# A plain output projection, kept up-projection operands, and down-projection operands made earlier

## The chip, the core and the metric

The kernel runs on one core of a Trainium2 chip. A core has a matrix engine (TensorE, PE in the rows; PEld is its loading of weights), three engines for elementwise work (VectorE or DVE, ScalarE or ACT, GpSimd or POOL), a sequencer SP that issues the DMAs here, and 16 DMA engines that move data between device memory and the on-chip memory SBUF. Matrix products land in PSUM, a small accumulator memory. Each engine runs its own list of instructions in order; semaphores tie them together. The metric is the time of one execution on the device in microseconds (us); lower is better.

## The reference

One encoder layer on two sequences, 512 and 2048 tokens of width 1024, all in fp32. The mixer concatenates four branches to a width of 1024; the change begins behind it:

```python
mix = jnp.concatenate([o_a, o_b, o_c, o_d], axis=-1)
return mix @ w_out                                        # (T, 1024) @ (1024, 1024)

def _conv_ffn(x, w_up, conv_w, conv_b, w_down):
    h = x @ w_up                                          # 1024 -> 2 * 2816
    hp = jnp.pad(h, ((0, 0), (1, 1), (0, 0)))
    h = hp[:, :-2] * conv_w[0] + hp[:, 1:-1] * conv_w[1] + hp[:, 2:] * conv_w[2] + conv_b
    gate, val = jnp.split(h, 2, axis=-1)
    return (jax.nn.gelu(gate) * val) @ w_down             # 2816 -> 1024

x = _layer_norm(ALPHA * x + mix, ln1_g, ln1_b)
x = _layer_norm(ALPHA * x + _conv_ffn(x, ...), ln2_g, ln2_b)
```

## The kernel before

**Split products.** A factor in fp32 is split into a high part, rounded to the matmul's input type (`hi`, on ACT), and a low part, the rest (`split`, line 131, on POOL or DVE). A product is three matmuls: high by high, high by low, low by high.

**Seven products for eight.** Output projection, up- and down-projection cut both factors into 2 x 2 blocks and form seven block products instead of eight. This needs sums and differences of blocks on both sides (`s1` to `s4`, `t1` to `t4`) and combination steps on the results. Each operand, a "unit" of 128 x 1024 (512 high and 512 low columns, 512 KB), is split on its own.

**Stages and order.** Order on each engine is not as written: a planner simulates the program and gives each engine the instruction of the highest priority (program order) that is ready, so work written later fills idle engines earlier. The order it finds is fixed in the program. All DMAs concerned are issued by SP.

1. Attention (`mla`), over 64 units of the sample and 16 of the prompt. At sample head two it calls `load_wout`; at steps 49, 67, 69, 81 and 82 of the loop in `build` the generator `outproj_head` makes more units of w_out and the first pair of mix tiles.
2. `outproj`: ten pairs of 128-token tiles. `mix_ops` loads two tiles of the mixed activations, forms four sums and differences, and splits seven operands into a ring of buffers (`op_ring`). `project` runs seven products of 12 matmuls (line 1141), with combination steps on DVE, ACT and POOL between them (`scaled`, line 1147), and `norm` does the layer norm. Operands of w_out stand in the ring "w" (12 slots) and in arena slots.
3. `ffn_up`: three blocks of tokens (`FF_BLOCKS`: 896, 896 and 768 tokens; seven products of 450, 450 and 386 columns). At each block's start `operands` makes B and T from the layer-normed x2 (through the two "xs" buffers). Then for each of 22 feature tiles f, `weights(f)` loads two 512 KB pieces of w_up, forms `s1` to `s4` (POOL, DVE; line 1209), and splits seven units into "w"; `features` runs 84 matmuls (lines 1313 to 1315), PSUM evacuation on DVE and ACT, the convolution (`conv`, lines 1319 to 1321), the gelu and the product (1354), and stores g. All of `weights` is done again in each block.
4. `ffn_down`: six chunks of w_down, 4 units in the first, 14 in the others, run through twice, each time for five pairs of token tiles (start offsets of 0 or 1 chunk). In the first pass `weights` (with `plain_units`, and `plain_weights` in `down_head`) makes the units from w_down and stores them to the scratch tensor `wdops`; in the second pass `again` loads them. `gate` loads and splits the activations g of the next job; `product` has the matmuls (line 1530).

Of the kernel before, what the change touches and what calls it, by code (L numbers as in the profile page):

```python
# [9 lines left out]
F32 = mybir.dt.float32  # L10
# [23 lines left out]
TOK0 = (2048, 0)  # L34
XW = 900
# [66 lines left out]
class Builder:  # L102
# [65 lines left out]
    def build(self):  # L168
        tc, nc, I = self.tc, self.nc, self.I
        with tc.tile_pool(name="cst", bufs=1, reuse_waits="tile") as cst, tc.tile_pool(name="scr", bufs=1, space=bass.MemoryType.DRAM) as scr:  # L170
# [34 lines left out]
            self.wd = self.t(scr, [NF // 2, 7, P, D], "wdops")  # L205

            with tc.tile_pool(name="arena", bufs=1, reuse_waits="tile") as self.A:
# [11 lines left out]
                with tc.tile_pool(name="mls", bufs=2, reuse_waits="tile") as ms:  # L219
# [8 lines left out]
                    for i, _ in enumerate(mla):  # L228
                        if i in (49, 67, 69, 81, 82):
                            next(head)  # L230
# [811 lines left out]
    def wout_units(self, k, js, units, lo_eng="pool"):  # L1042
        H = D // 2
        add = self.add
        wo = self.I["w_out"][0].rearrange("(k p) (a n) -> p k a n", p=P, a=KD)
        load = lambda h: self.wraw(wo[:, h * KD // 2 + k]).rearrange("p k n -> p (k n)")
        r1 = load(0) if js != (4,) else None
        r2 = load(1)
        b21, b22 = r2[:, :H], r2[:, H:]
        x = {4: b21, 6: b22}  # L1050
        if r1 is not None:
            b11, b12 = r1[:, :H], r1[:, H:]
            t1, t2, t3 = [self.t(self.wr2, [P, H], "s", bufs=4) for _ in range(3)]
            add("pool", t1, b12, b11, ALU.subtract)
            add("dve", t2, b22, t1, ALU.subtract)
            if 0 in js:
                add("pool", t3, b22, b12, ALU.subtract)
                x.update({0: b11, 1: t2, 2: t1, 3: t3})
            else:
                add("pool", t3, b21, t2, ALU.subtract)  # L1060
                x[5] = t3
        for j in js:
            u = units()
            self.split(x[j], u[:, :H], u[:, H:], "act", "dve" if lo_eng == "mix" and j % 2 == 0 else "pool")
            self.wout[k, j] = u

    def halves(self, slots, shape):
        for i in slots:
            t = self.a(i, [P, 2, D], F32R)
            for h in range(2):  # L1070
                yield t[:, h].rearrange(shape[0], **shape[1]) if shape else t[:, h]

    def load_wout(self):
        self.wout = {}
        self.wslot = self.halves((10, 12, 11, 9, 0, 5, 3, 4), None)
        for k in range(3):
            self.wout_units(k, (0, 1, 2, 3), lambda: self.wtile().rearrange("p k n -> p (k n)"))

    def mix_ops(self, p):
        KH = KD // 2  # L1080
        add = self.add
        raw = []
        for t in (2 * p, 2 * p + 1):
            s, i = (1, t) if t < 16 else (0, t - 16)
            raw.append(self.wraw(self.mix[s].rearrange("(k p) t -> p k t", p=P)[:, :, i * P:(i + 1) * P]))
        a11, a12, a21, a22 = raw[0][:, :KH], raw[0][:, KH:], raw[1][:, :KH], raw[1][:, KH:]
        s1, s2, s3, s4 = [self.t(self.wr2, [P, KH, P], "s", bufs=4) for _ in range(4)]
        add("pool", s1, a21, a22, ALU.add)
        add("dve", s2, s1, a11, ALU.subtract)
        add("pool", s3, a11, a21, ALU.subtract)  # L1090
        add("dve", s4, a12, s2, ALU.subtract)
        for i, x in enumerate((a11, s2, s1, s3, a12, a22, s4)):
            o = next(self.ops)
            self.split(x, o[:, 0], o[:, 1], "act", "pool" if i in (0, 4) else "dve")
            yield o

    def op_ring(self):
        KH = KD // 2
        while True:
            for tag in ("xs", "xs", "wraw2", "wraw2"):  # L1100
                yield self.t(self.wr2, [P, 2, KH, P], tag, F32R, bufs=2)
            yield from self.halves((7, 8, 2), ("p (h k e) -> p h k e", dict(h=2, k=KH)))

    def outproj_head(self):
        self.ops = self.op_ring()
        self.wout_units(3, (0, 1, 2, 3), lambda: next(self.wslot), "pool")
        yield
        for k in range(KD // 2):
            self.wout_units(k, (4,), lambda: next(self.wslot), "pool")
        yield  # L1110
        self.first = self.mix_ops(0)
        self.G0 = list(self.first)
        yield
        for k in range(KD // 2):
            self.wout_units(k, (5, 6), lambda: next(self.wslot), "mix")
            if k % 2:
                yield

    def outproj(self, head):
        nc, I, pp, add = self.nc, self.I, self.pp, self.add  # L1120
        H, KH = D // 2, KD // 2
        with self.tc.tile_pool(name="p3", bufs=2, reuse_waits="tile") as sp:
            G = {0: self.G0}
            place = lambda t: (1, t) if t < 16 else (0, t - 16)

            def fetch(p):
                P1[p] = self.t(sp, [P, H], "p1")
                x = self.a((1, 6)[p % 3 - 1], [P, 2, D]) if p % 3 else self.t(sp, [P, 2, D], "x", bufs=1)
                for h in range(2):
                    s, i = place(2 * p + h)  # L1130
                    self.load(x[:, h], self.y1[s][i * P:(i + 1) * P])
                return x
            P1 = {}
            X = {0: fetch(0)}
            next(head, None)
            W = self.wout

            def product(ps, G, i, first, last):
                for k in range(KH):
                    u = W[k, i]  # L1140
                    mm = lambda a, b, st, sp_: nc.tensor.matmul(ps, a, b, start=st, stop=sp_, skip_group_check=True)
                    mm(G[i][:, 0, k], u[:, :H], first and k == 0, False)
                    mm(G[i][:, 0, k], u[:, H:], False, False)
                    mm(G[i][:, 1, k], u[:, :H], False, last and k == KH - 1)

            def scaled(a, ps):
                nc.vector.scalar_tensor_tensor(a, a, ALPHA, ps, op0=ALU.mult, op1=ALU.add)

            def norm(t, x, late):
                s, i = place(t)  # L1150
# [4 lines left out]
                add("pool" if late else "dve", x, x, g_bc, ALU.mult)  # L1155
# [3 lines left out]
            def project(p):  # L1159
                x, g = X.pop(p), G.pop(p)  # L1160
                (x11, x12), (x21, x22) = [(x[:, h, :H], x[:, h, H:]) for h in range(2)]
                a, b, c = [self.t(pp, [P, 512], tag, bufs=n) for tag, n in (("s", 3), ("t", 3), ("o", 2))]
                e = "pool" if p < NP - 1 else "dve"
                product(a, g, 0, True, False)
                p1 = P1.pop(p)
                nc.scalar.copy(p1, a)
                product(b, g, 1, True, False)
                scaled(x12, b)
                product(c, g, 2, True, False)
                product(b, g, 3, False, False)  # L1170
                scaled(x22, b)
                add(e, x12, x12, p1, ALU.add)
                scaled(x21, p1)
                product(a, g, 4, False, True)
                scaled(x11, a)
# [495 lines left out]
```

## Time and profile before

| | us |
|---|---|
| three runs, median | 3377.93 |
| lowest and highest | 3365.83, 3380.04 |
| the profiled execution, whole | 3381.85 |
| its span, first to last instruction | 3379.5 |

| engine | busy us | share of the span |
|---|---|---|
| PE | 3164.6 | 94% |
| PEld | 2733.5 | 81% |
| DVE | 2486.9 | 74% |
| POOL | 2158.8 | 64% |
| ACT | 1526.9 | 45% |

DMA moved 405.84 MB, 120 GB/s on average. [...] A listed matmul duration overlaps the next ones, so the rate is read from the distance of starts. The shares are means over stages, so the stages are read one by one: 1315 to 1580 us is the output projection, 1583 to 1984, 1984 to 2387 and 2388 to 2774 us are the three feature blocks, and from about 2775 us on the down-projection runs.

### The profile page before, as it was taken

Reading aid. Unit: us, or ns where it says so; the run is one execution under the profiler, and the core shown is the slowest. Engines: PE = TensorE matmul, PEld = TensorE weight load, DVE = VectorE, ACT = ScalarE, POOL = GpSimd, SP = SyncE. Lnnn points to the kernel's source line nnn. Section 1 sums busy time; section 2 is a strip of 40 time slices with the busy share of each in tenths; the row PEclk is TensorE's granted clock in tenths of the full one; section 3 lists DMA queues with packets and bytes.
Section 4 is the critical chain, followed back from the end, with each engine's and each line's share of the span. In section 5 each row is a group of like instructions: output and inputs, shape, how many; then the busy total and the mean of one; then the engine's idle time right before and its main releaser. Section 6 shows DMA issues by size and latency. Waiting matters only on the chain. (4 is left out here: it accounts for less than half of the span.)

```text
span 3379.5 us, 45596 instructions
## 1 busy us (share of the span) xinstructions
PE 3164.6 (94%) x15999; PEld 2733.5 (81%) x15999; DVE 2486.9 (74%) x4000; ACT 1526.9 (45%) x2765; POOL 2158.8 (64%) x1651
## 2 busy tenths in 40 slices
PE   7899999799999997987999999999899988999997
PEld 6788878677889996765899979999799986777885
DVE  6332216676888887898788788887788778989768
ACT  3212215455677766333444454444444443444224
POOL 6322222345766657666888868888688868885546
PEclk9999999777999998998999999999899999999998
DMA  6222143523211004344322232222232248557653
GB/s 216 95 79 88 55 143 124 180 78 100 84 29 30 26 18 138 132 151 139 89 90 90 90 101 86 88 93 87 90 97 91 87 174 308 214 194 286 231 197 111
DMA packets 358465, 405.84 MB, mean 120 GB/s; under 512 B 42840, under 2 KB 286392, under 8 KB 356700
## 3 DMA queue, kind: packets, MB, share of 16 engines
q1 hardware_dynamic: 358236, 402.93, 36.0%
q8 instruction: 126, 2.06, 0.2%
q14 instruction: 103, 0.84, 0.1%
HBM read 269.02 MB, written 133.84 MB: 119 GB/s over the span
## 5 line engine op out<-in xcount | busy, mean ns | idle before, releaser
L131 POOL TENSOR_TENSOR w<-s,w 128x512 fp32r<-128x512 f32 x281 | 460.8, 1649 | 144.0 <-ACT w L121 140.3
L131 POOL TENSOR_TENSOR w<-wraw,w 128x512 fp32r<-128x512 f32 x189 | 277.9, 1479 | 42.5 <-ACT w L121 39.4
L1313 PE MATMUL t<-T,w 128*128 128x450 f32 (+1 forms) x792 | 286.9, 365 | 18.3 <-DVE u L1209 18.2
L1313 PE MATMUL s<-B,w 128*128 128x450 f32 (+1 forms) x792 | 286.2, 363 | 6.7 <-DVE h L1209 5.7
L1314 PE MATMUL t<-T,w 128*128 128x450 f32 (+1 forms) x792 | 286.9, 362 | 0.0
L1315 PE MATMUL t<-T,w 128*128 128x450 f32 (+1 forms) x792 | 286.8, 362 | 0.0
L1314 PE MATMUL s<-B,w 128*128 128x450 f32 (+1 forms) x792 | 286.1, 361 | 0.2 <-DVE B L131 0.2
L1315 PE MATMUL s<-B,w 128*128 128x450 f32 (+1 forms) x792 | 285.5, 360 | 0.0
L121 ACT CAST w<-wraw 128x512 fp32r<-128x512 f32 x225 | 138.2, 617 | 240.2 <-PE t L1315 142.8
L1320 DVE SCALAR_TENSOR_TENSOR h<-h,convc,h 128x896 f32<-128x896 f32 (+1 forms) x132 | 207.1, 1583 | 53.4 <-ACT h L1319 53.4
L1321 DVE SCALAR_TENSOR_TENSOR h<-h,convc,h 128x896 f32<-128x896 f32 (+1 forms) x132 | 239.9, 1839 | 0.0
L121 ACT CAST w<-s 128x512 fp32r<-128x512 f32 x299 | 183.5, 619 | 112.4 <-PE s L1315 54.9
L924 DVE TENSOR_SCALAR_CACHE_REDUCE a<-s,low 128x512 f32<-128x512 f32 x272 | 195.1, 745 | 31.7 <-PE t L952 23.9
L139 PE MATMUL mm<-xTl,a 128*128 128x512 f32 x520 | 205.7, 396 | 1.5 <-DVE xTl L131 1.5
L1530 PE MATMUL t<-w,go 128*128 128x512 f32 x696 | 195.8, 400 | 11.3 <-DVE xs L1371 4.8
L140 PE MATMUL mm<-xTh,a 128*128 128x512 f32 x520 | 201.7, 391 | 0.0
L138 PE MATMUL mm<-xTh,a 128*128 128x512 f32 x520 | 198.0, 394 | 1.4 <-ACT xTh L121 0.7
L131 DVE TENSOR_TENSOR a<-t,a 128x512 fp32r<-128x512 f32 x240 | 160.6, 682 | 32.5 <-ACT a L121 32.0
L1313 PEld LDWEIGHTS t<-T,w 128*128 128x128 f32 x792 | 151.5, 191 | 33.6 <-DVE u L1209 22.9
L940 POOL TENSOR_SCALAR a<-a,mrc 128x2048 f32<-128x2048 f32 (+1 forms) x80 | 140.0, 1752 | 49.5 <-DVE mrc L939 49.4
L121 ACT CAST a<-t 128x512 fp32r<-128x512 f32 x240 | 135.1, 586 | 79.7 <-PE t L952 74.5
L952 PE MATMUL t<-ident,a 128*128 128x128 f32 x1088 | 159.9, 278 | 10.1 <-DVE a L131 5.4
(412 smaller groups left out, 9574.7 us busy)
## 6 DMA issues: line engine op xcount, KB each, us to landing
wraw<-in_w_up_dram SPq DMA_DIRECT2D x132, 512.0 KB
w<-wdops SPq DMA_DIRECT2D x54, 512.0 KB
wdops<-w SPq DMA_DIRECT2D x50, 512.0 KB
graw<-g SPq DMA_DIRECT2D x100, 256.0 KB
g<-h SPq DMA_DIRECT2D x44, 448.0 KB
x<-x SPq DMA_DIRECT2D x24, 512.0 KB
wdops<-wd SPq DMA_DIRECT2D x24, 512.0 KB
wd<-wdops SPq DMA_DIRECT2D x24, 512.0 KB
```

Of the source, the lines that this page charges most:

```text
L121: nc.scalar.copy(out, src)
L131: e.tensor_tensor(lo, src, hi.bitcast(F32), op=ALU.subtract)
L138: mm(ps, wh, xh, start=first, stop=False)
L139: mm(ps, wh, xl, start=False, stop=False)
L140: mm(ps, wl, xh, start=False, stop=last)
L924: nc.vector.tensor_scalar(e[:, c * 512:c * 512 + 512], ps, 1.0, self.low, op0=ALU.mult, op1=ALU.max, accum_out=m4[:, c:c + 1])
L1313: mm(ps[:, :hw], a, xh[:, k, :hw], start=first and k == 0, stop=False, skip_group_check=True)
L1314: mm(ps[:, :hw], a, xl[:, k, :hw], start=False, stop=False, skip_group_check=True)
L1315: mm(ps[:, :hw], b, xh[:, k, :hw], start=False, stop=last and k == KH - 1, skip_group_check=True)
L1320: nc.vector.scalar_tensor_tensor(c[:, :n], hb[:, 1:n + 1], cw[:, 1, ft:ft + 1], c[:, :n], op0=ALU.mult, op1=ALU.add)
L1321: nc.vector.scalar_tensor_tensor(c[:, :n], hb[:, 2:n + 2], cw[:, 2, ft:ft + 1], c[:, :n], op0=ALU.mult, op1=ALU.add)
L1530: mm = lambda a, b, st, sp_: nc.tensor.matmul(ps, a, b, start=st, stop=sp_, skip_group_check=True)
```

## The change

- *Output projection.* Plain: `load_wout` loads eight pieces of w_out and splits sixteen units (twelve in "w", four in arena slots 10 and 12). `mix_ops(t)` loads one tile and splits it in two halves, high on ACT, low on DVE and POOL, into one of three arena slots. `project(t)` does 2 x 8 x 3 matmuls in two PSUM banks and one scaled sum for each. The head runs at steps 81 and 82 only.
- *Up-projection.* In block one `weights` also stores five of its seven units (1, 2, 3, 5, 6) to a new scratch tensor `wuops`. In blocks two and three `weights_again` loads these five into "w", and splits only units 0 and 4, from one loaded piece of w_up.
- *Down-projection operands.* The generator `down_ops` makes the 74 units of w_down in blocks two and three, two for each feature tile, through the two "xs" buffers, high on ACT, low on POOL, and stores them to `wdops`. `ffn_down` and `down_head` load units from there in both passes.

```diff
 def load_wout(self):
+    rest = self.halves((10, 12))
+    for k in range(KD):
+        raw = flat(self.wraw(wo[:, k]))
+        for h in range(2):
+            u = flat(self.wtile()) if k < 6 else next(rest)
+            self.split(raw[:, h * H:(h + 1) * H], u[:, :H], u[:, H:], "act", "pool")
+            self.W[k, h] = u
 def mix_ops(self, t):
+    raw = self.wraw(self.mix[s].rearrange("(k p) t -> p k t", p=P)[:, :, i * P:(i + 1) * P])
+    o = self.a((8, 9, 11)[t % 3], [P, 2, KD, P], F32R)
+    for h in range(2):
+        ks = slice(h * KD // 2, (h + 1) * KD // 2)
+        self.split(raw[:, ks], o[:, 0, ks], o[:, 1, ks], "act", ("dve", "pool")[h])
 def project(t):
+    for h in range(2):
+        for k in range(KD):
+            u = W[k, h]
+            self.mm3(ps[h], g[:, 0, k], g[:, 1, k], u[:, :H], u[:, H:], k == 0, k == KD - 1)
+        a = x[:, h * H:(h + 1) * H]
+        nc.vector.scalar_tensor_tensor(a, a, ALPHA, ps[h], op0=ALU.mult, op1=ALU.add)
+    norm(t, x)
 def weights(f):
+    if i in KEPT:
+        self.store(self.wu[f, KEPT.index(i)], u.bitcast(F32).rearrange("p k n -> p (k n)"))
+def weights_again(f):
+    g = self.wraw(wup[:, :, f * P:f * P + P])
+    for i in range(7):
+        u = self.wtile()
+        if i in KEPT:
+            self.load(u.bitcast(F32).rearrange("p k n -> p (k n)"), self.wu[f, KEPT.index(i)])
+        else:
+            h = slice(0, KH) if i == 0 else slice(KH, KD)
+            self.split(g[:, h], u[:, :KH], u[:, KH:], "act", "pool")
 for f in range(NF):
-    W = weights(f)
+    W = weights_again(f) if bi else weights(f)
+    if bi:
+        next(down_ops, None)
+        next(down_ops, None)
+def down_ops(self):
+    for k in range(FH):
+        for h in range(2):
+            raw.append(self.t(self.wr2, [P, KD, P], "wraw2", bufs=2))
+            self.load(raw[h], self.wdown(h * FH + k))
...
+            add("pool", t1, b12, b11, ALU.subtract)
+            add("dve", t2, b22, t1, ALU.subtract)
+            add("pool", t3, b22, b12, ALU.subtract)
+            add("dve", t4, b21, t2, ALU.subtract)
+        for i, x in enumerate((b11, t2, t1, t3, b21, t4, b22) if k else (b11, b12, b21, b22)):
+            o = self.t(self.wr2, [P, D], "xs", F32R, bufs=2)
+            self.split(x, o[:, :H], o[:, H:], "act", "pool")
+            self.store(self.wd[k, i], o.bitcast(F32))
+            yield
 def prepare(i):
+    for k in chunks[i % NC]:
+        for j in range(7 if k else 4):
+            got[i, k, j] = self.down_unit(unit(), k, j)
+            yield
```

## Rows read from the trace of the kernel before

**Rows 1.** Busy time by stage: stretch, length, PE, PEld, DVE, ACT, POOL, PEclk, DMA.

```profile
1345.00:1582.00 237.00, 203.10 (x815) 158.29 (x814) 211.11 (x270) 74.80 (x123) 148.98 (x83) 0.93 0.44 147
...
1620.00:1984.00 364.00, 363.75 (x1775) 332.56 (x1774) 301.69 (x264) 170.41 (x258) 297.15 (x187) 1.00 0.28 88
1984.00:2024.00 40.00, 32.99 (x146) 26.25 (x145) 27.57 (x54) 21.87 (x40) 26.93 (x22) 0.83 0.41 125
2024.00:2387.00 363.00, 362.07 (x1764) 330.89 (x1763) 300.20 (x266) 167.66 (x255) 294.82 (x185) 1.00 0.28 88
...
2428.00:2754.00 326.00, 306.98 (x1677) 303.14 (x1676) 261.67 (x249) 150.78 (x248) 276.29 (x175) 0.97 0.29 87
2754.00:2830.00 76.00, 59.25 (x254) 47.72 (x252) 59.70 (x77) 27.34 (x58) 49.55 (x43) 0.89 0.86 330
2830.00:3110.00 280.00, 266.73 (x1115) 209.92 (x1114) 259.56 (x397) 125.16 (x295) 221.12 (x214) 0.99 0.67 242
3110.00:3330.00 220.00, 220.00 (x946) 177.33 (x945) 162.35 (x279) 72.58 (x185) 122.78 (x150) 1.00 0.54 195
```

**Rows 2.** Timeline of PE, output projection: start, us, instruction, count, [idle before <-releaser].

```profile
1315.78 2.86 PE L1141 MATMUL s<-w,xs 128*128 128x512 f32 x9
...
1371.32 2.97 PE L1141 MATMUL t<-a,wraw 128*128 128x512 f32 x12
...
1379.67 2.27 PE L1141 MATMUL s<-w,a 128*128 128x512 f32 x9
...
1574.49 5.49 PE L1141 MATMUL o<-a,a 128*128 128x512 f32 x12 [3.81 <-DVE x L1371]
```

**Rows 3.** Waits of PE, 1345 to 1582: us in total, times, longest.

```profile
PE t L1141 <- DVE x L1147: 11.5, 4, 9.6
```

**Rows 4.** Groups of DVE, 1330 to 1590: busy us, mean ns | idle before.

```profile
L131 DVE TENSOR_TENSOR a<-s,a 128x512 fp32r<-128x512 f32 x23 | 29.5, 1282 | 0.0
L1371 DVE TENSOR_TENSOR a<-a,ln1g 128x1024 f32<-128x1024 f32 x12 | 20.2, 1682 | 5.3 <-ACT a L1154 5.2
L152 DVE BATCH_NORM_STATS2 ln1st<-a 128x6 f32<-128x512 f32 x24 | 15.8, 682 | 0.2
...
L1147 DVE SCALAR_TENSOR_TENSOR a<-a,t 128x512 f32<-128x512 f32 x12 | 8.1, 675 | 3.9 <-PE t L1141 3.9
```

**Rows 5.** Timeline of SP's DMA issues, start of the attention and its end.

```profile
862.86 2.61 SPq L113 DMA_DIRECT2D wraw<-in_w_out_dram  x2
...
1294.58 2.29 SPq L113 DMA_DIRECT2D wraw<-mix  x2
```

**Rows 6.** 1303 to 1345: all engines, then line 1141 alone.

```profile
1303.00:1345.00 42.00, 30.69 (x153) 25.61 (x152) 31.39 (x56) 23.19 (x49) 30.84 (x29) 0.83 0.42 133
...
1303.00:1345.00 42.00, 12.93 (x41) 9.54 (x42) 0.83 0.42 133
```

**Rows 7.** Groups of POOL and DVE in 18 feature tiles of block three, 2441.9 to 2739.0.

```profile
L131 POOL TENSOR_TENSOR w<-s,w 128x512 fp32r<-128x512 f32 x72 | 119.3, 1667 | 32.6 <-ACT w L121 32.6
...
L1209 POOL TENSOR_TENSOR s<-wraw,wraw 128x512 f32<-128x512 f32 x18 | 27.1, 1506 | 0.8
...
L1209 DVE TENSOR_TENSOR s<-wraw,s 128x512 f32<-128x512 f32 x18 | 23.1, 1285 | 14.8 <-POOL w L131 14.8
```

**Rows 8.** Timeline of PE in block three, a run and a pause.

```profile
2550.21 0.34 PE L1313 MATMUL t<-T,w 128*128 128x386 f32 x1
...
2554.63 0.34 PE L1313 MATMUL t<-T,w 128*128 128x386 f32 x1
...
2559.38 0.57 PE L1313 MATMUL t<-T,w 128*128 128x386 f32 x1 [2.30 <-DVE u L1209]
```

**Rows 9.** Busy time: 10 us after that pause; 30 us of the down-projection's start.

```profile
2560.00:2570.00 10.00, 10.00 (x50) 10.00 (x50) 5.44 (x7) 4.00 (x6) 7.78 (x6) 0.85 0.45 138
...
2790.00:2820.00 30.00, 23.94 (x86) 17.46 (x85) 24.82 (x30) 7.99 (x21) 24.97 (x24) 0.80 1.03 412
```

**Rows 10.** Waits of ACT, 1600 to 2780: us in total, times, longest.

```profile
ACT w L121 <- PE t L1315: 171.4, 99, 5.8
```

More of the change, by code (lines that the diff above doesn't have):

```diff
@@ L34 @@
 TOK0 = (2048, 0)
+KEPT = (1, 2, 3, 5, 6)
 XW = 900
@@ L228, in build @@
                     for i, _ in enumerate(mla):
-                        if i in (49, 67, 69, 81, 82):
-                            next(head)
+                        if i in (81, 82):
+                            next(head, None)
                 self.outproj(head)
@@ L1040, in wraw, with load_wout, halves @@
         return raw
-    def wout_units(self, k, js, units, lo_eng="pool"):
+    def load_wout(self):
         H = D // 2
-        add = self.add
+        self.W = {}
         wo = self.I["w_out"][0].rearrange("(k p) (a n) -> p k a n", p=P, a=KD)
[L1046 to L1067, printed above, removed]
+        flat = lambda a: a.rearrange("p k n -> p (k n)")
+        rest = self.halves((10, 12))
[5 more added lines that the diff above has]
+                self.W[k, h] = u
+    def halves(self, slots):
         for i in slots:
@@ L1070, in halves @@
             for h in range(2):
[L1071 to L1102, printed above, removed]
-    def outproj_head(self):
[L1105 to L1117, printed above, removed]
+                yield t[:, h]
@@ new lines, in place, with mix_ops @@
+    def place(self, t):
+        return (1, t) if t < 16 else (0, t - 16)
+    def mix_ops(self, t):
+        s, i = self.place(t)
+        raw = self.wraw(self.mix[s].rearrange("(k p) t -> p k t", p=P)[:, :, i * P:(i + 1) * P])
[3 more added lines that the diff above has]
+            self.split(raw[:, ks], o[:, 0, ks], o[:, 1, ks], "act", ("dve", "pool")[h])
+        return o
+    def outproj_head(self):
+        self.G = {}
+        for t in range(2):
+            self.G[t] = self.mix_ops(t)
+            yield
@@ L1119, in outproj @@
     def outproj(self, head):
         nc, I, pp, add = self.nc, self.I, self.pp, self.add
-        H, KH = D // 2, KD // 2
+        H = D // 2
         with self.tc.tile_pool(name="p3", bufs=2, reuse_waits="tile") as sp:
[L1123 to L1150, printed above, removed]
@@ L1154, in norm @@
                 nc.scalar.activation(x, x, AF.Identity, bias=nr, scale=r)
-                add("pool" if late else "dve", x, x, g_bc, ALU.mult)
+                add("dve", x, x, g_bc, ALU.mult)
                 add("pool", x, x, b_bc, ALU.add)
                 self.store(self.x2[s][i * P:(i + 1) * P], x)
[L1159 to L1175, printed above, removed]
-                add(e, x22, x22, p1, ALU.add)
-                add("dve", x22, x22, c, ALU.add)
-                product(b, g, 5, False, True)
-                add("dve", x21, x21, b, ALU.add)
-                product(c, g, 6, False, True)
-                add("dve", x12, x12, c, ALU.add)
-                for h in (1, 0):
-                    norm(2 * p + h, x[:, h], p == NP - 1)
@@ L1191, in outproj @@
+            fetch(0)
+            for t in range(NT):
+                if t + 1 < NT:
+                    fetch(t + 1)
+                    if t + 1 not in G:
+                        G[t + 1] = self.mix_ops(t + 1)
+                if t == 0:
                     g_bc = self.t(sp, [P, D], "ln1g", bufs=1)
@@ L1361, in ffn_up @@
             meta = {}
+            down_ops = self.down_ops()
             for bi in range(len(FF_BLOCKS)):
@@ L1404, in down_head @@
         wr2 = self.wr2
-        self.head_w = self.plain_weights(self.wtile)
+        self.head_w = [self.down_unit(self.wtile(), 0, i) for i in range(4)]
         raw = self.t(wr2, [P, 2, 1, 2 * P], "wraw2", bufs=2)
```

90 lines of the change are left out of this document (27 added, 63 removed).

## The prediction

> **What bounds the kernel now.** I read the busy time by stage first, since the share over the whole span hides which stage is limited by what. The reader should see two kinds of stage [rows 1]. In feature blocks one and two (1620 to 1984, 2024 to 2387) and in the second pass of the down-projection (3110 to 3330) PE is busy all the time at full clock: only fewer or shorter matmuls would help there. In the output projection (1345 to 1582), block three (2428 to 2754) and the first pass of the down-projection (2830 to 3110) PE has holes, at a mean clock under 1, while DVE or POOL is at 80 to 94%. Only these three can pay for the change.
>
> To price the holes I take the matmul pitch from the timeline. A listed duration overlaps its neighbours, so I use starts: 36 matmuls of 512 columns take 1379.67 - 1371.32 = 8.35 us, 0.232 us each [rows 2]. In block three (386 columns) 25 matmuls take 2554.63 - 2550.21 = 4.42 us, 0.177 us each [rows 8]. A stage's loss is its length less count times pitch.
> - Output projection: 840 x 0.232 = 195 us of matmuls, between a first group at 1315.8 and an end at 1574.49 + 5.49 = 1580.0 [rows 2].
> - Block three: 326 - 1677 x 0.177 = 29 us lost [rows 1].
> - Down-projection, first pass: 280 - 1115 x 0.232 = 21 us lost; second pass: 220 - 946 x 0.232 = 0.5 us [rows 1].
>
> Who is late: in the output projection PE's longest waits are for DVE, 9.6 us [rows 3] and 3.8 us before the last group [rows 2]; DVE has 211 us of work in 237 [rows 1]. In block three the chain is one step longer. POOL does nine operations of 128x512 a feature tile (seven low parts, two sums) at 1.5 to 1.7 us: 13.6 to 15.0 us, against 84 x 0.177 = 14.9 us of matmuls; with what it waits for, 18 tiles take 297 us, 16.5 us a tile. DVE's two differences wait for POOL (14.8 us in the 18 tiles) [rows 7], the PSUM evacuation stands behind them on DVE, and PE waits 2.3 us for it, after which a matmul is listed with 0.57 us instead of 0.34 [rows 8].
>
> **The change, part by part.**
>
> *Plain output projection.* Seven products become eight: 20 tiles x 2 halves x 8 x 3 = 960 matmuls instead of 840, so +120 x 0.232 = +27.8 us on the engine that is the bound nearly everywhere. Against that stands what leaves DVE. A plain tile asks of it two scaled sums from PSUM (0.675), two statistics (0.682), one gain (1.68), one low half (1.28) and some small ones [rows 4]: 5.7 us and a little, against 48 x 0.232 = 11.1 us of matmuls. Six of seven combination steps, the four operand differences a pair and most low parts are gone; POOL, at 149 of 237 us [rows 1], loses work too. So I expect this stage to be bound by PE, without holes.
>
> Its start: the 16 weight operands are asked for at head two of the attention, but the planner runs such work far ahead; the loads of w_out begin at 862.9 [rows 5]. The old ones took eighteen POOL operations (twelve low parts, six differences) and three of DVE; the new ones take sixteen low parts on POOL and none of DVE. So it is nothing; the two saved, some 3 us, are one end, and the other, if planned worse, as much again. The operand units made in the attention's tail go. The first mix columns are loaded at 1294.6 [rows 5]; a tile needs only a load and two splits. By my estimate that is some 8 us, so that products begin at 1303; the ends are 1.3 us for 512 KB at the rate of [rows 9] and a split of 1.3 us [rows 4], and the 21 us that the old units took from there to the first group at 1315.8 [rows 2]. From 1303 to 1345 PE is busy 30.7 us, of which 41 projection matmuls take 41 x 0.232 = 9.5 us [rows 6]: 21 us of attention remain. End: 1303 + 21 + 960 x 0.232 = 1547, against 1580: -33. I take **-30**, for a pause or two. Bounds: -33 - 5 with the early start, -20 with the late one, and +28 if the old holes stay.
>
> *Into each block.* Each f = 0 takes some 20 us more than a tile, because DVE, ACT and the x2 loads make the operands B and T (1984 to 2024: PE 33 of 40 us, clock 0.83) [rows 1]. This work stays. It gains from fewer splits beside it, and loses because the x2 loads now share two "xs" buffers and the queue with stores. I take **0**, -3 to +6 for each of three.
>
> *Block one* gets five stores of 512 KB a tile. They need SP and the DMA engines, both with room (88 GB/s, share 0.28 [rows 1]); a slot of the 12-slot ring "w" is free only when its store has landed too, but the product that frees it comes later anyway. **0**; behind a store on SP stand the next raw loads, a tile ahead, so a delay under some 15 us costs nothing.
>
> *Blocks two and three.* Five of seven operands come by load, two are split from one raw half; two units of w_down are made a tile. POOL a tile: 2 + 2 low parts and 4/7 of a sum, 4.6 operations x 1.6 = 7.3 us instead of 13.6 to 15.0. DVE loses two differences and gets 4/7 of one. Block two is at PE's limit already: **0**. Block three's holes come from POOL, so they go: **-28** of 29. What is late next there is PE itself; DVE has 262 us in 326 [rows 1] and loses more than a tenth of it. Bounds: -29, 0.
>
> The change adds waits here. SP's loads into "w" wait for PE to release a slot. Behind them stand the g stores, the stores of w_down units and raw loads; ACT (line 1319, which reuses the "h" buffer of a g store; and the casts into "xs", two buffers, each free when its store has landed) waits for those. A slot is reused twelve products later, 12 x 12 x 0.177 = 25 us in block three: that is the cover, and its failing is the slow rival below.
>
> DMA volume a tile in block three: 0.5 MB raw w_up, 2.6 operands, 1.0 stores, 0.3 w_down, 0.4 g = 4.9 MB, over 14.9 us 330 GB/s; in block two, over 17.3 us, 287. The trace shows 412 GB/s for 30 us with PE at work beside it [rows 9], so it fits.
>
> *Down-projection.* Its first pass makes no operands any more: 14 loads a chunk replace four raw loads, splits and 14 stores. That is the second pass's work, which loses 0.5 us. I take **-18** of 21; the rest are epilogues. Bounds: -21, 0. At the start (2754 to 2830, PE 59 of 76 us at 330 GB/s [rows 1]) fourteen operand loads now go ahead of the gate loads, where two raw pairs stood; 6 more loads of 512 KB at 412 GB/s [rows 9] are 7.6 us, against splits saved: **0**, -10 to +12.
>
> **Sum.** -30 - 28 - 18 = -76 us. The profiled execution took 3381.85 us (span 3379.5), so 3306; it lies 3.9 us above the median of the three, 3377.93, so the forecast for a median is **3302 us**.
>
> **The rivals.**
> - *The matmuls are added, the holes stay.* Plain tiles still wait (small DVE operations, the mix loads). For: the stage is not in this form in the trace. Against: DVE would be half idle. +28 instead of -30: 3360.
> - *Block three and the first pass keep their holes*, because DVE, not POOL, set them. For: PE's waits name DVE [rows 8]. Against: DVE's own waits there name POOL [rows 7]. +46: 3348.
> - *DMA becomes the bound.* The planner bunches the w_down units, since POOL is free: at seven a tile in block two, 8.3 MB a tile, at 412 GB/s [rows 9] 20.2 us against 17.3, 2.9 us for each of 74/7 = 10.6 tiles: +31, 3333. [...]
> - *Slower: ACT stands still for a store.* Each of the 74 units casts into one of two "xs" buffers; ACT runs in order, and the copies that PE's next product on the bank needs stand behind the cast. If the store is late (SP is behind a load that waits for PE), PE pauses. Price of one pause: 2.3 us [rows 8] and the slower matmuls after it (50 in 10 us where 10/0.177 = 56 fit [rows 9]), 1.1 us: 3.4 us. From 76/3.4 = 22 of 74 pauses on the gain is gone; with half of them, +126: 3428. For: ACT waits 171 us for PE at the same casts already [rows 10]. Against: those waits, up to 5.8 us, leave blocks one and two without a loss [rows 1]. [...]
> - *The change doesn't do what it says*: the loads come too late to replace the splits. It is the slow rival's cousin, priced within it.
>
> **How the numbers follow.** Forecast 3302 (own range 3280 to 3325, from the bounds of transitions and start): 0.60. DMA-bound, 3333: 0.09. Holes kept in block three and first pass, 3348: 0.09. Holes kept in the projection, 3360: 0.07. Transitions and start gain too, 3302 - 9 - 10 = 3283 or somewhat less: 0.06. Slow, 3428: 0.09. The range that leaves out 2 in 10 is 3268 to 3350. Over 0.5% (17 us, about what a measurement of this kernel tells from no change) faster is below 3361: 0.85 (half of the case at 3360 among it). Same, the rest of that case and the tail of the one at 3348: 0.06. Slower: 0.09.
>
> **What would show it.** Output projection: some 960 matmuls, 223 us of them, at clock 1, DVE under 65%. Block three: 14.9 us a tile, POOL under 55%, no wait of PE for DVE over 1 us. First pass: PE over 98%. Wrong would be: PE waits on line 1313 in blocks two and three with ACT's casts into "xs" waiting for DMA; a DMA share of 1 in block two with PE holes; PE waits for mix loads or DVE in the projection; a first f of a block over 42 us.

## The result

The changed kernel takes 3291.48 us (median of 4 runs, 3286.28 to 3299.96), the kernel before 3378.98 (median of 4, 3365.83 to 3380.87): a ratio of 0.9752, 95% interval 0.9718 to 0.9785, 87.5 us less. The forecast was 3302, with a range of 3268 to 3350. The profiled execution of the changed kernel took 3299.96 us (span 3298.2, mean granted clock of TensorE 0.962 of full speed; before 0.953), the longest of its four; by the prediction's sum it should have been 3306.

In the profiles, the attention's first score matmul starts at 847.7 us before and at 852.7 after. In the profiles of the runs below, whose edits all lie behind it, it starts between 837.0 and 846.8. What happens ahead of it says nothing on the change, so I take times from that matmul on (starts of matmuls in the timelines of PE; for the projection the end of its last one):

| from the first score matmul to | before | after | difference | this step | predicted |
|---|---|---|---|---|---|
| the projection's end | 732.3 | 688.9 | -43.4 | -43.4 | -30 |
| second feature tile of block one | 772.0 | 735.9 | -36.1 | +7.3 | 0 |
| block two | 1136.7 | 1099.8 | -36.9 | -0.8 | 0 |
| its second tile | 1175.0 | 1133.5 | -41.5 | -4.6 | 0 |
| block three | 1540.0 | 1498.3 | -41.7 | -0.3 | 0 |
| its second tile | 1579.3 | 1541.4 | -37.9 | +3.8 | 0 |
| its last up-projection matmul | 1926.6 | 1857.0 | -69.6 | -31.7 | -28 |
| the end of the span | 2531.8 | 2445.4 | -86.4 | -16.8 | -18 |

These are two profiles, and single steps vary between profiles of the same code. In three runs below that keep the old projection it ends at 726.2 to 727.1 us, and in the runs with the plain one (but for one that puts work into the attention) at 686.0 to 688.9, so its step is -37 to -46. The first feature tile of block one, 37.2 and 45.2 us here, takes 34.8 to 35.0 and 44.1 to 46.3 us there.

The changed kernel by stage, the stages of [rows 1] and [rows 6] again (stretch, length, busy us and count of PE, PEld, DVE, ACT and POOL, granted clock of TensorE as a share of full speed, DMA share, GB/s):

```profile
1303.00:1345.00 42.00, 42.00 (x228) 35.98 (x227) 22.54 (x54) 17.93 (x37) 8.53 (x11) 0.98 0.28 88
1345.00:1541.00 196.00, 196.00 (x843) 157.83 (x842) 98.85 (x166) 51.41 (x77) 73.95 (x39) 1.00 0.47 153
1541.00:1589.00 48.00, 31.95 (x161) 25.81 (x160) 30.60 (x64) 22.69 (x45) 32.98 (x27) 0.82 0.71 216
1589.00:1952.00 363.00, 363.00 (x1774) 332.62 (x1773) 289.05 (x262) 166.51 (x252) 284.54 (x181) 1.00 0.69 242
1952.00:1986.00 34.00, 27.82 (x131) 22.44 (x130) 20.31 (x42) 20.06 (x37) 23.23 (x22) 0.90 0.62 203
1986.00:2351.00 365.00, 365.00 (x1782) 334.21 (x1782) 231.16 (x240) 138.02 (x194) 152.87 (x98) 1.00 0.82 290
2351.00:2394.00 43.00, 31.25 (x134) 25.36 (x133) 19.97 (x43) 18.24 (x36) 20.28 (x20) 0.72 0.50 155
2394.00:2710.00 316.00, 316.00 (x1785) 315.26 (x1784) 192.69 (x231) 116.86 (x178) 107.03 (x73) 1.00 0.86 300
...
2760.00:3030.00 270.00, 264.62 (x1117) 210.70 (x1116) 211.16 (x362) 102.22 (x248) 151.75 (x174) 0.99 0.65 233
3030.00:3250.00 220.00, 219.12 (x940) 176.10 (x939) 161.42 (x279) 72.00 (x180) 117.78 (x144) 1.00 0.54 192
```

The reader is to see PE busy without a hole, at clock 1.00, in the projection (196 of 196 us, DVE at 50% instead of 89) and in block three (316 of 316, POOL at 34% instead of 85). What is left are three short stretches, the first f of each block, where PE is busy for 32 of 48, 28 of 34 and 31 of 43 us at clocks from 0.72 to 0.90. PE's waits there, at the start of block one and then of block three (us in total, times, longest):

```profile
PE s L1258 <- DVE B L132: 6.4, 1, 6.4
PE t L1198 <- DMA xs<-x: 5.9, 1, 5.9
PE o L1198 <- DVE o L1196: 2.1, 1, 2.1
...
PE t L1198 <- DMA xs<-x: 7.9, 3, 3.8
PE o L1198 <- DMA xs<-x: 3.0, 4, 2.1
PE t L1257 <- ACT T L122: 0.9, 1, 0.9
```

### The profile page after: what moved, and what is told of

The parts are those of the page before. It is cut to its first block, busy times and chain, and to the rows that moved or that the text cites. A ratio compares the mean times of both kernels' runs of the same rounds, so it can differ in the third digit from the quotient of the medians.

```text
span 3298.2 us, 45978 instructions
## 1 busy us (share of the span) xinstructions
PE 3152.9 (96%) x16119; PEld 2739.0 (83%) x16119; DVE 2130.4 (65%) x3770; ACT 1390.7 (42%) x2493; POOL 1617.3 (49%) x1329
## 4 chain that ended last, share of the span: by engine, by line
PE 84%; DVE 6%; DMA 5%; ACT 2%; issue 2%; SPq 1%; POOL 1%; DVEq 0%; ACTq 0%; POOLq 0%
PE s L1257 6%; PE s L1258 6%; PE s L1259 6%; PE t L1452 6%; PE t L1257 5%; PE t L1258 5%; PE t L1259 5%; PE s L139 4%; PE s L1452 4%; PE s L140 4%; PE s L141 4%; PE o L1452 4%; PE t L954 3%; PE mm L141 3%; PE mm L140 3%; PE mm L139 3%
## 5 line engine op out<-in xcount | busy, mean ns | idle before, releaser
L132 POOL TENSOR_TENSOR w<-wraw,w 128x512 fp32r<-128x512 f32 x162 | 235.5, 1459 | 315.1 <-ACT w L122 269.4
L1258 PE MATMUL t<-T,w 128*128 128x450 f32 (+1 forms) x792 | 283.8, 358 | 0.0
L1259 PE MATMUL t<-T,w 128*128 128x450 f32 (+1 forms) x792 | 283.7, 358 | 0.0
L1257 PE MATMUL t<-T,w 128*128 128x450 f32 (+1 forms) x792 | 282.1, 360 | 0.9 <-ACT T L122 0.9
L1265 DVE SCALAR_TENSOR_TENSOR h<-h,convc,h 128x896 f32<-128x896 f32 (+1 forms) x132 | 215.2, 1661 | 0.0
L1264 DVE SCALAR_TENSOR_TENSOR h<-h,convc,h 128x896 f32<-128x896 f32 (+1 forms) x132 | 168.9, 1310 | 50.7 <-ACT h L1263 50.7
L1263 ACT ACTIVATE h<-h,convc 128x896 f32<-128x896 f32 (+1 forms) x132 | 138.3, 1096 | 133.3 <-DVE h L1138 130.8
L132 DVE TENSOR_TENSOR a<-t,a 128x512 fp32r<-128x512 f32 x240 | 161.1, 682 | 35.3 <-ACT a L122 34.7
L122 ACT CAST w<-wraw 128x512 fp32r<-128x512 f32 x166 | 102.1, 618 | 191.9 <-PE t L1259 132.7
L1452 PEld LDWEIGHTS t<-w,go 128*128 128x128 f32 x696 | 131.1, 189 | 39.5 <-DVE x L1319 4.0
L1258 PEld LDWEIGHTS s<-B,w 128*128 128x128 f32 x792 | 150.7, 190 | 15.4 <-DVE B L132 6.7
L122 ACT CAST go<-gs 128x256 fp32r<-128x256 f32 x200 | 78.2, 405 | 196.8 <-PE t L1452 65.2
```

Of the source, the lines that this page charges most:

```text
L122: nc.scalar.copy(out, src)
L132: e.tensor_tensor(lo, src, hi.bitcast(F32), op=ALU.subtract)
L1257: mm(ps[:, :hw], a, xh[:, k, :hw], start=first and k == 0, stop=False, skip_group_check=True)
L1258: mm(ps[:, :hw], a, xl[:, k, :hw], start=False, stop=False, skip_group_check=True)
L1259: mm(ps[:, :hw], b, xh[:, k, :hw], start=False, stop=last and k == KH - 1, skip_group_check=True)
L1265: nc.vector.scalar_tensor_tensor(c[:, :n], hb[:, 2:n + 2], cw[:, 2, ft:ft + 1], c[:, :n], op0=ALU.mult, op1=ALU.add)
```

## The experiments

Ratios are against the kernel before, run on the same chip beside them (medians 3374.77 to 3375.98 us).

**The parts alone.** First the plain projection in the kernel before (whole functions are exchanged; the edit in words):

```
-    # outproj_head, mix_ops, op_ring, wout_units: seven products
+    # load_wout: sixteen plain operands; outproj: eight products
     # weights(f) in all blocks, w_down operands in the first pass, as before
```

> The kernel before with the plain output projection alone; the feature blocks and the down-projection stay as before. Theory (PE bounds a plain projection): its last matmul lies 39 us earlier, as it does in the changed kernel (1541.4 against 1580.0), and the start of block one gives some 8 us of that back (its first f took 45.2 us there against 37.2), since it now follows the projection with nothing prepared; so about -31 us, ratio 0.991. Rival (the added matmuls count in full, the holes stay): 120 x 0.232 = +28 us. Rival (the projection's gain is a gain of the whole change and is lost alone, because the low parts of block one's weights are then late): -39 at the projection's end, under -10 at the end.

Measured: 3336.81 us, ratio 0.9893 (0.9877 to 0.9908), about -36 us. The projection's end lies at 686.3 us after the first score matmul (-46.0), the first f of block one takes 44.1 us instead of 37.2, and 38 us are kept at the end of the span. The theory holds, with some 5 us more than it gave. Of the rivals, +28 is excluded, and so is the loss of the whole.

Then the kept up-projection operands:

```
+                    if i in KEPT:
+                        self.store(self.wu[f, KEPT.index(i)], ...)
...
-                    W = weights(f)
+                    W = weights_again(f) if bi else weights(f)
```

> The kernel before with the kept up-projection operands alone: five stores a tile in block one, loads in place of five splits in blocks two and three. The w_down operands are made in the first pass of the down-projection as before, the output projection is the old one. Theory (POOL made block three's holes): 21 tiles of block three take 313 to 317 us instead of 347.4, blocks one and two 364 us as before, the first pass keeps its 21 us of holes; about -32 us, ratio 0.9905. Rival (DVE, which PE's waits name, made the holes): block three gains no more than the two differences that leave DVE, under 10 us. Rival (the gain of block three comes only with the w_down units moved into it): none.

Measured: 3341.21 us, ratio 0.9903 (0.9888 to 0.9918), about -33. Its block three, and its down-projection's first pass (busy time by stage, columns as above):

```profile
2418.00:2734.00 316.00, 316.00 (x1783) 315.22 (x1782) 183.68 (x223) 106.09 (x156) 67.34 (x46) 1.00 0.72 244
...
2800.00:3085.00 285.00, 270.30 (x1126) 210.55 (x1125) 261.85 (x400) 123.40 (x293) 219.57 (x214) 0.99 0.66 239
```

Block three's holes are gone without the w_down part: 315.9 us for its last 21 tiles, as in the changed kernel. POOL is at 21% (before: 85), but DVE has lost its two differences a tile too and is at 58% (before: 80), so this run does not tell the two engines apart; the runs with added POOL work below do. The first pass still has 15 us without a matmul (before: 13). The two parts together, -36 and -33, leave 15 us by the ratios for the third, the w_down operands, 14 by the medians. That is a difference of three measurements, each with an interval of 5 us or more to either side; no run has the first two parts without the third.

That third part alone, with all operands of w_up still split in every block:

```
                     W = weights(f)
+                    if bi and f % 4 == 0:
+                        next(down_ops, None)   # one whole k, up to seven units
```

> The kernel before with the w_down operands alone made during blocks two and three, while the up-projection operands are still split in every block (one whole k, four sevenths of a unit a tile, every fourth tile). The first pass of the down-projection loads them. Theory (POOL is what block three lacks): POOL gets some 2.6 operations of 1.6 us more a tile on average, 4.2 us; in block two 13.6 to 15 plus 4.2 passes the 17.3 us of matmuls by up to 2 us, in block three the 16.5 us by 2 to 4; so +40 to +110 us in the blocks, against -17 us in the first pass: slower, by +25 to +95 us. Rival (DVE sets block three's pace, POOL only follows): the first pass's -17 us comes and nothing is added, about -17 us.

Measured: 3481.01 us, ratio 1.0324 (1.0304 to 1.0344), +105 us. The last 21 tiles of blocks two and three take 435.9 and 401.0 us instead of 364.9 and 347.4, +125 together; from the last up-projection matmul to the end it is 584.8 us instead of 605.2. Block two's busy time, then PE's first wait in it and DVE's:

```profile
2009.00:2445.00 436.00, 386.04 (x1781) 344.36 (x1780) 332.65 (x283) 187.43 (x296) 384.97 (x237) 0.95 0.40 133
```

```profile
PE t L1328 <- DVE u L1211: 32.2, 15, 3.6
DVE s L1211 <- POOL s L1211: 42.0, 15, 6.8
```

POOL is at 88% and the stage that had no hole has 50 us of them, in which PE is said to wait for DVE, and DVE waits for POOL. ACT's waits for the stores out of "xs" are no longer than in the changed kernel (19.3 us; there 20.6, see below). So the w_down part pays only because the kept operands have emptied POOL first. My +95 as the upper end was too low by 10.

**DMA and ACT as the next bound.**

```
-                        next(down_ops, None)
-                        next(down_ops, None)
+                        for _ in range(7):
+                            next(down_ops, None)
```

> The changed kernel with up to seven w_down units a feature tile instead of two, so that all 74 are asked for in the first eleven tiles of block two. Theory (the planner and the queues spread the work; PE has priority): within 5 us of the changed kernel, about 3291 us. Rival one (DMA becomes the bound): 8.3 MB a tile, at 412 GB/s 20.2 us instead of 17.3, +31 us. Rival two (casts into the two raw buffers make ACT wait for stores, and PE for the copies behind them): pauses of 3.4 us, up to five a tile in these eleven tiles, over +60 us, and the trace shows PE waiting for the copies of a feature tile out of PSUM.

Measured: 3309.67 us, ratio 0.9811 (0.9794 to 0.9827): 18 us more than the changed kernel, outside the theory's 5, and by neither rival as written. Of the 74 units, 72 are stored by 2346 us, in the changed kernel 44. Block two, 20 us in it, and what follows it (busy time), then the first 220 us of block two in the changed kernel:

```profile
1977.00:2346.00 369.00, 365.65 (x1767) 334.84 (x1766) 252.48 (x242) 150.55 (x219) 207.46 (x131) 0.99 0.94 333
...
2017.00:2037.00 20.00, 20.00 (x99) 18.33 (x98) 13.95 (x14) 9.10 (x13) 9.76 (x8) 1.00 1.03 383
...
2346.00:2366.00 20.00, 3.49 (x13) 2.05 (x12) 7.51 (x11) 6.55 (x12) 4.25 (x3) 0.64 0.58 205
```

```profile
1986.00:2206.00 220.00, 220.00 (x1073) 201.74 (x1073) 150.66 (x142) 91.07 (x131) 125.44 (x79) 1.00 0.94 337
```

PE's first wait from 1977 to 2407, and SP's DMA issues there (start, us, count):

```profile
PE o L1198 <- DMA xs<-x: 19.1, 7, 13.5
```

```profile
2348.61 0.38 SPq L114 DMA_DIRECT2D wraw<-in_w_up_dram  x1
2354.01 0.32 SPq L117 DMA_DIRECT2D g<-h  x1
2355.13 1.54 SPq L117 DMA_DIRECT2D wdops<-xs  x2
2357.85 14.20 SPq L114 DMA_DIRECT2D xs<-x  x18
```

In the block, DMA's share is 0.94 and 333 GB/s, but PE loses only 4 us: units that find no room are put off, not PE. The changed kernel has the same share for 220 us, which its stage mean of 0.82 hides, and PE has no hole there. Whether DMA or the two buffers put the units off, this run does not separate. The price is paid at the block's end: the loads of x2 for block three need the same two "xs" buffers, and stand on SP behind the last two units' stores, which are issued at 2355.1; PE waits 13.5 us in one piece. The slow rival's mechanism (stores of units in "xs") exists, but it stops the next block's loads and not ACT's copies. In the changed kernel ACT does wait for these stores, and PE does not:

```profile
ACT xs L122 <- DMA wdops<-xs: 20.6, 16, 4.8
```

**POOL or DVE in block three.** Extra POOL subtractions a tile, whose results are not used, four and then eight:

```
+                    for _ in range(extra if i < 4 else 0):
+                        add("pool", self.t(self.wr2, [P, KH, P], "s", bufs=4), g[:, :KH], g[:, KH:], ALU.subtract)
...
-                    W = weights_again(f) if bi else weights(f)
+                    W = weights_again(f, 1 if bi == 2 else 0) if bi else weights(f)   # 2 for eight
```

> The changed kernel with four more POOL subtractions of 128x512 a feature tile in block three (extra work, of which nothing is used). POOL has 4.6 such operations a tile there now and is busy 36% of 315 us; 8.6 are 11 to 13.8 us, still under the 14.85 us that the matmuls of a tile take. Theory (POOL sets the pace as soon as its work passes the matmuls, and not before): no change, within 6 us. Rival (POOL's load slows DVE, whose operations took 1583 ns before and 1310 ns now, and DVE behind PE's waits sets the pace): 21 tiles lengthen already here, by 5 us or more, with PE waiting for DVE.

> The changed kernel with eight more POOL subtractions of 128x512 a feature tile in block three (extra work, of which nothing is used). 12.6 operations are 16.1 us at 1.28 us, 20 us at the 1.6 us they took in block three of the kernel before. Theory (POOL sets the pace): a tile takes 16.5 to 20 us instead of 14.85, so +36 to +110 us over 21 to 22 tiles. Rival (DVE, not POOL, sets it; the low parts have tiles of slack): under +15 us.

Measured: 3298.13 us (ratio 0.9773, 0.9760 to 0.9787) and 3360.36 (0.9955, 0.9941 to 0.9968), 7 and 69 us above the changed kernel. The last 21 tiles of block three take 327.9 and 386.2 us instead of 315.6 (315.6 to 319.0 in the changed kernel and the three runs below that leave these tiles as they are). Block three with four (busy time, then PE's first wait), then the same two with eight:

```profile
2386.00:2713.00 327.00, 317.30 (x1778) 313.48 (x1777) 231.41 (x231) 114.84 (x178) 240.26 (x152) 1.00 0.84 289
```

```profile
PE s L1259 <- DVE h L1138: 5.5, 4, 2.4
```

```profile
2389.00:2775.00 386.00, 336.03 (x1782) 326.34 (x1781) 253.84 (x231) 113.78 (x178) 355.79 (x233) 0.94 0.70 245
```

```profile
PE t L1259 <- DVE u L1138: 37.0, 12, 11.6
```

Eight bear the theory out: POOL at 92%, 18.4 us a tile, and again PE is said to wait for DVE, which has nothing more to do than in the changed kernel. Four go to the rival: POOL at 73% costs 9 to 12 us, where by the theory it should cost nothing. PE's waits there all name DVE, DVE waits for POOL nowhere, and its busy time rises from 193 to 231 us for the same instructions. DVE groups of block three in the kernel before (2441.9 to 2739), in the changed kernel and in the one with four extra operations (both 2400 to 2700; busy us, mean ns | idle before):

```profile
L1321 DVE SCALAR_TENSOR_TENSOR h<-h,convc,h 128x770 f32<-128x770 f32 x38 | 62.7, 1666 | 0.0
L1320 DVE SCALAR_TENSOR_TENSOR h<-h,convc,h 128x770 f32<-128x770 f32 x37 | 60.9, 1664 | 17.5 <-ACT h L1319 17.5
```

```profile
L1265 DVE SCALAR_TENSOR_TENSOR h<-h,convc,h 128x770 f32<-128x770 f32 x42 | 62.1, 1509 | 0.0
L1264 DVE SCALAR_TENSOR_TENSOR h<-h,convc,h 128x770 f32<-128x770 f32 x42 | 42.3, 1046 | 15.6 <-ACT h L1263 15.6
L1138 DVE TENSOR_TENSOR h<-s,u 128x386 f32<-128x386 f32 x41 | 22.8, 557 | 34.1 <-PE s L1259 33.8
```

```profile
L1267 DVE SCALAR_TENSOR_TENSOR h<-h,convc,h 128x770 f32<-128x770 f32 x40 | 71.8, 1830 | 0.0
L1266 DVE SCALAR_TENSOR_TENSOR h<-h,convc,h 128x770 f32<-128x770 f32 x40 | 58.8, 1505 | 16.3 <-ACT h L1265 16.3
L1138 DVE TENSOR_TENSOR h<-s,u 128x386 f32<-128x386 f32 x40 | 22.2, 556 | 27.2 <-PE s L1261 26.8
```

From the changed kernel to the one with four extra, the convolution's operations, whose tensors lie in SBUF, lengthen by 44 and 21%; the sums that read PSUM stay at 557 and 556 ns. Only POOL's work was added, so the lengthening comes with it; by what mechanism, these rows do not show. So POOL makes PE wait in two ways in these runs: by its own queue when it is nearly full (92% with eight), and before that (73% with four) by the longer operations on DVE beside it. The kernel before had 85% on POOL and its holes lie between those of the two runs: 32 us against 12 and 71. It has both ways at once: DVE's operations are long there (1666 and 1664 ns), and DVE waits for POOL (14.8 us before one of its differences [rows 7]); their shares in the 32 us are not shown.

**The start of a block.** The one load of 127 rows in two pieces:

```
-                                self.load(xs[h][:n, at], x2[row:row + n])
+                                c16 = n // 16 * 16 if n == P - 1 else n
+                                self.load(xs[h][:c16, at], x2[row:row + c16])
+                                if c16 < n:
+                                    self.load(xs[h][c16:n, at], x2[row + c16:row + n])
```

> The changed kernel with the one 127-row load of x2 at the start of a block split into 112 rows and 15 rows. In the changed kernel the issue of each 127-row load holds SP for 2.65 to 3.61 us, where the others take 0.25 to 0.4, and PE waits 7.9 + 3.0 us for loads of x2 at the start of block three. [...] Theory (the odd row count makes these loads late): the first f of block three takes 34 to 38 us instead of 43.0, about -6 us in all. Rival (the two raw buffers, free only when the transposes of the pair before are done, make the loads late): the issues get short, the first f of block three stays within 2 us, no change in all.

Measured: 3274.24 us (median of 5, 3267.91 to 3276.28), ratio 0.9701 (0.9688 to 0.9714): 17 us below the changed kernel, more than expected, and the fastest of all kernels here. (The other run on the start of a block, below, whose edit made no difference, took 3289.24 us beside it, 15 us more.) The first f of block three takes 31.9 us instead of 43.0. SP's issues in the changed kernel, the load of 127 rows and the next one, of 3 x 128 rows; then the three issues in their place with the split (112, 15 and 3 x 128 rows); then PE's waits at the start of block three with the split:

```profile
2346.15 0.24 SPq L114 DMA_DIRECT2D xs<-x  x1
...
2346.44 2.87 SPq L114 DMA_DIRECT2D xs<-x  x1
```

```profile
2328.97 1.42 SPq L114 DMA_DIRECT2D xs<-x  x3
```

```profile
PE s L1261 <- DVE B L132: 2.4, 1, 2.4
PE s L1261 <- POOL T L132: 1.0, 1, 1.0
PE t L1260 <- ACT T L122: 0.7, 1, 0.7
PE t L1201 <- DMA xs<-x: 0.2, 1, 0.2
```

PE's 10.9 us of waiting for these loads become 0.2. I had read the long issue as that of the 127-row load; it is that of the load behind it, which is held for 0.85 to 3.61 us behind 127 rows at the start of block three (kernel before and changed kernel), and takes 0.4 to 0.6 us behind the 15 rows of the split. So 127 rows are dear there and 112 + 15 are not; why, the runs do not show. Counted from the first score matmul, the end lies 17.5 us earlier than in the changed kernel: 11.1 from this stretch, 5.0 from behind the last up-projection matmul, 2.7 from ahead of block three, less 1.3 in block three. The 5.0 are not the split's: that stretch takes 583.4 us here, 582.8 to 586.0 in the other runs that make the w_down operands early, and 588.4 in the changed kernel's own profile. So 11 us are shown to be the split's, and the rest of the 15 to 17 is not placed.

The same split in the kernel before:

> The kernel before with the one 127-row load of x2 at the start of a block split into 112 rows and 15 rows, nothing else. In the changed kernel the split took the first f of block three from 43.0 to 31.9 us. Theory (the cost was there before the change, and is no part of it): the first f of block three goes from 39.2 to some 30 us, -8 us in all, ratio 0.9975. Rival (it costs only in the changed kernel, where the two raw buffers and the queue are shared with the w_down units): no change in the first f.

Measured: 3367.41 us (median of 10), ratio 0.9983 (0.9973 to 0.9994), -7 us. The first f of block three goes from 39.2 to 34.7, not to 30. The cost was there before; in the changed kernel it is more than twice as large (11.1 against 4.5), so theory and rival each hold half. The issue behind the 127 rows, at the start of block three, is held for 0.85 to 3.12 us in the kernel before, most often about 1, and for 0.99 to 3.61 in the changed kernel, most often about 2.8.

For block one, all low parts of the first two tiles' weights on POOL:

```
-                    self.split(x, u[:, :KH], u[:, KH:], "act", "dve" if f < 2 and i % 2 == 0 else "pool")
+                    self.split(x, u[:, :KH], u[:, KH:], "act", "pool")
```

> The changed kernel with the low parts of the weights of the first two feature tiles of block one all on POOL, where four of seven were on DVE. In the changed kernel PE waits 6.4 us for a low part of B that stands behind 12 us of such work on DVE, and the first f of block one takes 45.2 us where it took 37.2 before. Theory (that queue on DVE gives back the 8 us): the first f of block one takes 38 to 41 us, -4 to -7 us in all. Rival (POOL, with eight more operations of 1.3 to 1.75 us, is late with the weights and with the low parts of T): no gain, up to +5 us.

Measured: 3289.24 us, ratio 0.9744 (0.9731 to 0.9757), no difference from the changed kernel, and 46.3 us for the first f of block one. The theory of one queue falls. PE's waits there now:

```profile
PE t L1198 <- DMA xs<-x: 8.3, 1, 8.3
PE o L1198 <- DVE o L1196: 6.9, 1, 6.9
```

The wait for B is gone, and two others have grown from 5.9 and 2.1 us: for the loads of x2, and for a DVE operation that stands behind a sum which waits for POOL. The first f of block one wants low parts, sums and loads at once, and none of the three is alone in the way.

**The attention.** The changed kernel with the differences that the old w_out operands needed put back beside their loading:

```
+            if k < 3:
+                x1, x2, x3 = [self.t(self.wr2, [P, H], "s", bufs=4) for _ in range(3)]
+                self.add("pool", x1, raw[:, H:], raw[:, :H], ALU.subtract)
+                self.add("dve", x2, raw[:, H:], x1, ALU.subtract)
+                self.add("pool", x3, raw[:, H:], raw[:, :H], ALU.subtract)
```

> The changed kernel with six POOL and three DVE subtractions of 128x512 put beside the loading of the w_out operands, as many as the old operands had there (their results are not used). In the kernel before, the 680 us that follow the first score matmul of the attention hold some 16 us that neither the matmuls of the projection nor its holes account for: the second head takes 45.0 us there (76.5 - 31.5) against 41.0 in the changed kernel and 40.6 with the plain projection alone, and by the eighth twelfth of the scores the old kernel is 8.3 us behind. Theory (the operand differences take POOL and DVE away from the softmax of the second and third head): the attention is 5 to 10 us longer again by then, the median 5 to 10 us above 3291. Rival (the order of the loads, in pairs of raw columns, made it late): under 2 us. Theory and rival agree that the other 8 us, at the attention's end, where thirteen more operands and the first products' operands were made, do not come back.

Measured: 3293.53 us, ratio 0.9766 (0.9749 to 0.9783). In the profile eleven twelfths of the score matmuls are done at 407.8 us instead of 401.4 (before: 409.6), +6.4, and the span's end, counted from the first score matmul, is 6.8 us later: the theory's 5 to 10. The medians differ by 2 us, which two sessions of four runs do not resolve, so the place is shown and the size is not certain. The 50 us in question in the kernel before, then at the same distance from the first score matmul in the changed kernel and in this run:

```profile
880.00:930.00 50.00, 43.39 (x261) 37.32 (x259) 38.48 (x92) 33.33 (x53) 44.04 (x37) 0.93 0.21 74
```

```profile
885.00:935.00 50.00, 48.03 (x313) 41.99 (x312) 40.22 (x108) 37.92 (x62) 43.20 (x37) 0.97 0.21 69
```

```profile
869.30:919.30 50.00, 44.22 (x287) 37.74 (x286) 37.79 (x96) 36.65 (x57) 49.35 (x40) 0.99 0.22 74
```

PE gains 4.6 us in 50, in a stretch that belongs to the attention, and loses 3.8 of them again when the differences are back.

## Why the prediction was right, and where it was off

- *Output projection, -30: the mechanism holds, the term is 13.4 us too small in this pair of profiles.* The 120 added matmuls found the holes, as predicted: from the attention's last matmul to the projection's last it is 210.5 us instead of 238.1, -27.6. The step that failed is "its start", where the weight operands were put at "nothing", with 3 us as the bound. The attention's last value matmul ends 478.4 us after the first score matmul instead of 494.2: 8.2 of these 15.8 us are gained by the time eleven twelfths of the score matmuls are done, 7.6 behind it. I had counted POOL and DVE operations as two fewer, and not asked who stands behind them: the softmax of the second and third heads. And I had written that the operand units of the attention's tail "go", without a price; [rows 6] had it, PE busy 30.7 of 42 us, now 42.0. For the first part the added differences show the cause; that these units cost the other 7.6 us is argued, no run tested it.
- *Into each block, 0 each, -3 to +6: the sum holds, the single ones do not.* +7.3, -4.6 and +3.8 make +6.5. The sign that I had named as wrong, a first f over 42 us, came twice (45.2 and 43.0). Block one now follows the projection with less prepared, which no run tested by itself; block three's loads of x2 share their buffers and queue, as I had said, and the size was off because I had not looked at the shape of these loads.
- *Blocks one and two, 0 each:* -0.8 and -0.3. The stores and loads, DMA at 242 and 290 GB/s (predicted 287 in block two), cost nothing.
- *Block three, -28:* -31.7. 14.85 us a tile (predicted 14.9), POOL at 34%, no wait of PE for DVE. That POOL's work makes such holes is shown by the extra operations, and that the edit takes them away by the kept operands alone; what I had not seen is that POOL makes them through DVE's durations too, a second reason for PE's waits to name DVE as in [rows 8]. The rival that DVE sets the pace was in part true, and the same edit cures it.
- *First pass, -18, and the start of the down-projection, 0:* -16.8 together. PE is at 98% in the first pass. In other runs with the w_down part the stretch behind the last up-projection matmul is 582.8 to 586.0 us, against 588.4 in this profile and 605.2 before, so -17 to -22.
- *The DMA rival* does not come, nor at seven units a tile: block two then takes 3.9 us more, not 31, since the units spread over the whole block. The 412 GB/s of [rows 9] was not reached there: block two's stretches of 20 us with a DMA share of 1.01 to 1.03 moved 350 to 383 GB/s in the changed kernel, and 383 in the 20 us shown above with seven units a tile, so the rate that the price rested on did not show in this mix of loads and stores.
- *The slow rival* does not come in the form that I gave it: ACT waits 20.6 us for stores out of "xs", and PE none of it in the tiles. It comes where two users of "xs" meet, at the start of a block, and costs 18 us when the units are still running there.
- *The total* came out closer than its terms, and that is in part luck: 13.4 us too small in the projection and 3.7 in block three, against 6.5 lost at the starts of the blocks that I had put at 0.

## What to carry to other kernels

Before putting work on an engine with room, look at what the change takes off it first: the w_down operands cost 105 us alone and gain some 15 once the kept operands have emptied POOL. When a stage's work is removed, price it at every stage in which it had been issued, not where it is used; here a third of the projection's gain lay in the attention. Two users of one small ring of buffers collided here at the seam between stages, where PE waited 13.5 us in one piece, so read the first tile of each stage by itself, shapes of the loads included.

## What was new of the hardware

- With more POOL work beside them, DVE's operations on SBUF tensors took longer in block three, and those that read PSUM did not: 128x770 at 1046 and 1509 ns with POOL at 34%, 1505 and 1830 ns at 73%; 557 and 556 ns for the sums from PSUM.
- Behind a load of 127 rows, itself issued in 0.24 us, the next issue on the queue took 2.87 us; with 112 and 15 rows in its place all three issues together took 1.42 us. By the medians the split gave 15 to 17 us in the changed kernel and 7 in the kernel before; 11.1 and 4.5 of them are shown at the first feature tile of block three.
